# A hybrid decoder layer on one core: three ties in the order of its feed-forward tiles

## The chip, the core and the metric

The kernel runs on one core of a Trainium2 chip. Its engines are TensorE (PE in the profile, with PEld for the loading of weights into the array), VectorE (DVE), ScalarE (ACT), GpSimd (POOL) and SyncE (SP). The last two issue transfers here. The metric is the device time of one execution in microseconds (us). Three executions of the kernel before took 1223.24, 1223.34 and 1223.8 us; the median is 1223.34 us.

## What is computed

One decoder layer on 512 tokens of width 1024 in float32: a SwiGLU feed-forward (width 2816), a pair of token mixers with a gated merge, and a second SwiGLU feed-forward, each with a norm before and behind it.

```python
def swiglu(x, w_gate, w_up, w_down):
    return (jax.nn.silu(x @ w_gate) * (x @ w_up)) @ w_down

f = swiglu(rms_norm(h, ffn1_norm_pre[l]), ffn1_w_gate[l], ffn1_w_up[l], ffn1_w_down[l])
h = h + 0.5 * rms_norm(f, ffn1_norm_post[l])
u = rms_norm(h, mix_norm_pre[l])
...
h = h + rms_norm(merged @ w_out[l], mix_norm_post[l])
f = swiglu(rms_norm(h, ffn2_norm_pre[l]), ffn2_w_gate[l], ffn2_w_up[l], ffn2_w_down[l])
h = h + 0.5 * rms_norm(f, ffn2_norm_post[l])
```

The change touches the first feed-forward and the entry into the second; the mixers between them stay as they are.

## The kernel before

**Products.** Every operand is split into a high and a low part (`split`, lines 268 to 270: ACT copies the high part, DVE subtracts it for the low part), and a product of two operands is three matmuls: high by high, high by low, low by high. The 22 tiles of 128 feed-forward columns are numbered f. The first 6 (in the second feed-forward the first 3) are computed directly (`std`). Each of the others is computed by `prod` (line 994): gate and up weights against the two halves of the tokens form a two by two block product that needs seven products instead of eight, p1, p5, p6, p2, p7, p3, p4 in this order, with 12 matmuls of 256 columns each (lines 1008 to 1010). The weights of a tile come as one transfer (`raw`) and are summed and split by `w_forms_in_place` (line 646) into four tiles: p1 and p2 share one, p7 and p5 another, p6 and p3 a third, p4 has its own.

**Banks.** In `prod`, `b` is the accumulator bank of p1, p6, p7 and p4 (bank 0 for even f, bank 1 for odd f), `y` is bank 2 and `z` is bank 5. Behind p1, ACT copies b into y (line 1029); behind p5 it copies z away as `c5` and behind p6 b as `c6` (line 1016). p3 adds onto z and must wait until c5 was read; DVE then forms the two sums of line 1021: for the up half, b behind p7 plus c5 (the **up sum**), and for the gate half, z behind p3 plus c6 (the **gate sum**). p4 adds onto b and must wait for the up sum.

**Down parts.** The product with the down weights is computed in groups of four tiles, again by seven products, here called down parts: `step` (line 913) runs one of them, 12 matmuls of 512 columns (lines 922 to 924) in two halves of 6, on banks 3 and 4 or 6 and 7. `ffn_order` (line 55) places them behind tiles; in the first feed-forward the table `LEAD` (line 26) puts three down parts in a row (p1, p2, p5) behind tiles 7 and 10, and two behind tiles 8, 9, 11 and 12. The weights of a down part are brought by `supply` (line 885) on POOL's queue into `npair` or into one of two `dr` tiles, and split into `wd` by `down_form` (line 897). For p6 and p3 the transfer adds onto what `npair` holds, so it can only be issued once the part before it in `npair` was split. In `prod`, the splits for the coming down parts are tied behind the last ACT copy, c6 (`with behind("copy")`, line 1037).

**What sets the order.** The program is recorded in the order of the code and then put in order by priorities; a high priority pulls an instruction ahead. `behind(...)` (line 987) ties the instructions recorded inside it behind the last one noted for an engine in the dictionary `last`. p1 of every tile is tied behind the last PE instruction recorded before (line 1024), a down part likewise; p5 and p3 are not tied and can be pulled ahead. The weight forms of a coming tile (`prep`) are tied behind DVE's and ACT's last noted instructions; the dictionary is empty when a feed-forward starts.

**Between the feed-forwards.** The last product of the mixers (`last_product`, line 439) works on four blocks of 128 tokens. For each, `Boundary.block` (line 473) computes the new h, its squared sum on ACT (line 478), the root with a few operations on single columns (lines 390 and 342 to 344) and the normed rows u (line 483). `Boundary.turn` (line 487) transposes u on PE (line 491), and ACT and DVE split it into the inputs of the second feed-forward (lines 494 to 496). `gemm_first` (line 305) runs the first five direct products of the second feed-forward, first for the first 256 tokens, then for the others; `turn(2)` stands behind its third product and `turn(3)` behind its fourth.

Of the kernel before, what the change touches and what calls it, by code (L numbers as in the profile page):

```python
# [10 lines left out]
F32 = mybir.dt.float32  # L11
F32R = mybir.dt.float32r
AF = mybir.ActivationFunctionType
# [12 lines left out]
LEAD = {7: (0, ("p1", "p2", "p5")), 8: (0, ("p6", "p7")), 9: (0, ("p3", "p4")),  # L26
        10: (1, ("p1", "p2", "p5")), 11: (1, ("p6", "p7")), 12: (1, ("p3", "p4"))}
# [127 lines left out]
def hybrid_layer(ctx: ExitStack, tc: tile.TileContext, xT: bass.AP, xN: bass.AP, wst: bass.AP,  # L155
                 first: bass.AP, rows: bass.AP, wdn: bass.AP, wbig: bass.AP, consts: bass.AP, bias: bass.AP, out: bass.AP):
    nc = tc.nc
    DVE, ACT, PE = nc.vector, nc.scalar, nc.tensor
# [30 lines left out]
    def fb(b, sl=slice(0, D)):  # L189
        return facc[:, 2 * b:2 * b + 2, :].rearrange("p k t -> p (k t)")[:, sl]  # L190
# [219 lines left out]
    FHALVES = (slice(0, T), slice(T, D))  # L410
# [54 lines left out]
    class Boundary:  # L465
# [21 lines left out]
        def turn(self, b):  # L487
            for i, u in enumerate(self.u.pop(b)):
                ps = aux_ps()
                for j in range(4):  # L490
                    PE.transpose(ps[:, j * P:(j + 1) * P], u[:, j * P:(j + 1) * P], ident)
                src = ps.rearrange("p (k t) -> p k t", k=4)
                hi, lo = (t[:, :, b * P:(b + 1) * P] for t in (self.his[i], self.los[i]))
                ACT.activation(hi, src, AF.Copy)
                DVE.tensor_sub(lo, src, hi.bitcast(F32))
                ACT.activation(fb(b, FHALVES[i]), ps, AF.Copy)

    def act_of(his, los):
        return Act([his[k // 4][:, k % 4, :] for k in range(8)], [los[k // 4][:, k % 4, :] for k in range(8)])
# [57 lines left out]
    def forms_of(x, his, los, pool, copied, places={}):  # L557


        spool[0] = pool  # L560
        fx = facc.rearrange("p k t -> p (k t)").rearrange("p (b c) -> p b c", b=4)

        def quarter(i, j):
            return fx[:, 2 * j:2 * j + 2, i * T:i * T + T]

        def slot():
            return tx_slot(pool, 1 if copied else 2).rearrange("p s k t -> p s (k t)").rearrange(
                "p s (b c) -> p s b c", b=2)

        x01, x10, x11 = quarter(0, 1), quarter(1, 0), quarter(1, 1)  # L570
        t, d = {}, {}
        for name, i, j in (("p1", 0, 0), ("p2", 1, 0), ("p3", 1, 1)):
            t[name] = tuple(z[i][:, :, HALVES[j]] for z in (his, los))

        def copies():
            for name in ("p1", "p2", "p3"):
                v = big([P, 2, 4, HB])
                for i in range(2):
                    nc.gpsimd.dma_start(v[:, i], t[name][i])
                t[name] = v[:, 0], v[:, 1]  # L580

        def form(name, v, src):
            t[name] = tuple(v[:, i].rearrange("p b (k t) -> p k b t", k=4) for i in range(2))
            split(v[:, 0], v[:, 1], src)

        def first():
            d[1], d[2] = (pool.tile([P, 2, T], F32, name="ts", tag="s", bufs=2) for _ in range(2))
            DVE.tensor_sub(d[1], quarter(0, 0), x01)
            DVE.scalar_tensor_tensor(d[2], x11, -1.0, d[1], op0=ALU.mult, op1=ALU.subtract)
            form("p6", slot(), d[2])  # L590

        def second():
            DVE.tensor_sub(x01, x11, x01)
            form("p7", places["p7"](), x01)

        def third():
            DVE.scalar_tensor_tensor(d[2], d[2], -1.0, x10, op0=ALU.mult, op1=ALU.subtract)
            form("p4", slot(), d[2])

        def fourth():  # L600
            form("p5", places["p5"](), d[1])

        if not copied:
            return t, [first, second, third, fourth]

        def early():
            if copied:
                copies()
            d[1], d[2] = (pool.tile([P, 2, T], F32, name="ts", tag="s", bufs=2) for _ in range(2))
            DVE.tensor_sub(d[1], quarter(0, 0), x01)  # L610
            DVE.scalar_tensor_tensor(d[2], x11, -1.0, d[1], op0=ALU.mult, op1=ALU.subtract)
            DVE.tensor_sub(x01, x11, x01)

        def middle():
            form("p6", slot(), d[2])
            DVE.scalar_tensor_tensor(d[2], d[2], -1.0, x10, op0=ALU.mult, op1=ALU.subtract)
            form("p5", big([P, 2, 2, T]), d[1])

        def late():
            form("p7", big([P, 2, 2, T]), x01)  # L620
            form("p4", big([P, 2, 2, T]) if copied else slot(), d[2])

        return t, [early, middle, late]
# [189 lines left out]
        def rows(self):  # L813
            return self.ub.rearrange("p (s k) t -> p s (k t)", s=2)

    def ffn(n, x, r, forms_x, home, pss):
        t, steps = forms_x
        n0 = NSTD[n]
        ub, wdt, dr = home.ub, home.wd, home.dr
# [161 lines left out]
                    else:  # L981
                        add(u0, True)

        last = {}

        @contextmanager
        def behind(*engines):
            with ExitStack() as es:
                for e in engines:
                    if e in last:  # L990
                        es.enter_context(tc.issue_after(last[e]))
                yield

        def prod(f, w, due):

            g = tmp("g")
            b, y, z = b_of[f % 2][:, :HB], y_[:, :HB], z_[:, :HB]
            u = ub[:, f % 4, :] if 4 < f < LAST[0] or f < 4 else tmp("u")
            if n == 1 and f in (6, 8):
                u = tmp("u")  # L1000

            def product(p, ps, start):
                if len(t[p][0].shape) == 4:
                    ps = ps.rearrange("q (b t) -> q b t", b=2)
                for k in range(4):
                    ks = slice(k * P, (k + 1) * P)
                    wh, wl, xh, xl = w[p][:, 0, ks], w[p][:, 1, ks], t[p][0][:, k], t[p][1][:, k]
                    PE.matmul(ps, wh, xh, start=start and k == 0, stop=False, skip_group_check=True)  # L1008
                    PE.matmul(ps, wh, xl, start=False, stop=False, skip_group_check=True)  # L1009
                    i = PE.matmul(ps, wl, xh, start=False, stop=k == 3, skip_group_check=True)  # L1010
                last["PE"] = i.ins

            def copy(ps):
                c = tpool.tile([P, HB], F32, name="c", tag="c", bufs=CB)
                with tc.high_priority(offset=EVAC):
                    last["copy"] = ACT.activation(c, ps, AF.Copy).ins  # L1016
                return c

            def sum_of(dst, ps, c):
                with tc.high_priority(offset=EVAC):  # L1020
                    DVE.tensor_add(dst, ps, c)

            lead = f == n0
            with behind("PE"):
                product("p1", b, True)
            c1 = copy(b) if lead else None
            if not lead:
                with tc.high_priority(offset=EVAC):
                    ACT.activation(y, b, AF.Copy)
            product("p5", z, True)  # L1030
            c5 = copy(z)
            product("p6", b, False)
            c6 = copy(b)
            product("p2", y, lead)
            if lead:
                sum_of(g[:, lo_], y, c1)
            with behind("copy"):
                for a, p in due:
                    down_form(a, p)
            product("p7", b, False)  # L1040
            sum_of(u[:, hi_], b, c5)
            with tc.high_priority(offset=EVAC):
                ACT.activation(g[:, lo_], g[:, lo_] if lead else y, AF.Silu)
            product("p3", z, False)
            sum_of(g[:, hi_], z, c6)
            product("p4", b, False)
            last["ACT"] = ACT.activation(g[:, hi_], g[:, hi_], AF.Silu).ins
            with tc.high_priority(offset=EVAC):
                DVE.scalar_tensor_tensor(u[:, lo_], g[:, lo_], -1.0, b, op0=ALU.mult, op1=ALU.mult)
            last["DVE"] = DVE.scalar_tensor_tensor(u[:, hi_], g[:, hi_], -1.0, u[:, hi_], op0=ALU.mult,  # L1050
                                                   op1=ALU.mult).ins
            return u
# [76 lines left out]
        last = Act(*zip(*(last_act(f) for f in range(*LAST))))  # L1129
# [16 lines left out]
    pss = [acc_ps() for _ in range(4)]  # L1146
# [36 lines left out]
    with ExitStack() as mx:  # L1183
# [17 lines left out]
        pss = [acc_ps() for _ in range(4)]  # L1201
# [209 lines left out]
        early = dpool.tile([2 * len(AHEAD_PAIRS), P, T], F32, name="early")  # L1411
        ready = {}
        for i, (c, kind) in enumerate(AHEAD_PAIRS):
# [6 lines left out]
            f = AF.Sigmoid if kind == "sig" else AF.Gelu_apprx_tanh  # L1420
# [7 lines left out]
    with ExitStack() as mx:  # L1428
# [130 lines left out]
        for hd in range(NH):  # L1559
# [9 lines left out]
            for kind, c in FILL[hd]:  # L1569
                if kind == "attn":  # L1570
                    ws = fetch((kind, c))
                    for i in range(2):
                        ps = acc_ps()
                        gemm(ps, [w[:, i * T:(i + 1) * T] for w in ws], attn)
                        DVE.tensor_mul(facc[:, 2 * c + i, :], ps, facc[:, 2 * c + i, :])
                else:
                    ps = acc_ps()
# [10 lines left out]
        for c in range(KC):  # L1588
            ps = acc_ps()
# [7 lines left out]
    home2 = Home(ap2)  # L1597
# [8 lines left out]
    keys = [(w, 2, i) for i in range(NSTD[2]) for w in ("gate", "up")]  # L1606
    pss = gemm_first(keys[:NFIRST], u2, [home2.spare()[2]],
                     {3: [lambda: bd2.turn(2)], 4: [lambda: bd2.turn(3)]})
    end2 = ffn(2, u2, None, forms_of(u2, his, los, ap2, True), home2, pss)
    new_h()  # L1610
    for b in range(4):
        nc.gpsimd.dma_start(hb(b), kept[b])
# [132 lines left out]
```

## Time and profile before

| | |
|---|---|
| median of three executions | 1223.34 us |
| profiled execution, its own time | 1223.28 us |
| span of its instructions | 1221.2 us (2.1 us lie around it) |
| granted TensorE clock | 0.999 |
| DVE | 984.0 us busy, 81% |
| ACT | 746.0 us busy, 61% |
| raw weights, SP queue | 90 transfers of 1024 KB, 4.9 us from issue to landing (median) |
| `npair`, POOL queue | 32 transfers of 512 KB, 5.5 us (median) |
| `dr`, POOL queue | 40 transfers of 512 KB, 5.8 us (median) |

Busy shares are averages over very different stages. PE's records overlap, since a matmul is pipelined: the distance from one start to the next tells what a matmul costs, not the length of its record. Where the start-to-start distance is longer than usual, PE waited, and the bracket at the end of a row names the idle time that is left and what ended it.

### The profile page before, as it was taken

What the parts mean: (1) busy time and instruction counts of PE and PEld (TensorE: products, weight loads), DVE (VectorE), ACT (ScalarE), POOL (GpSimd) and SP (SyncE); (2) the same over time, 40 slices, a digit from 0 to 9 for tenths busy, and PEclk for the clock granted to TensorE, in tenths of its full rate; (3) what the DMA queues carried; (4) which work ended last, traced back from release to release, by engine and by line L of the source; (5) the groups of instructions that cost most, each with busy time, mean ns of one, the idle gap of its engine ahead of it and who ended that gap; (6) DMA issues with size and microseconds to landing.
All of it is one profiled execution on the core that took longest, in us unless ns stands there. A gap on an engine that the chain in (4) does not pass through costs nothing.

```text
span 1221.2 us, 19573 instructions
## 1 busy us (share of the span) xinstructions
PE 1209.9 (99%) x7790; PEld 1102.6 (90%) x7790; DVE 984.0 (81%) x1540; ACT 746.0 (61%) x1238; POOL 84.5 (7%) x139
## 2 busy tenths in 40 slices
PE   9999999999999999999999999999999999999998
PEld 8898989999878899999999888888899999999996
DVE  7998878988579888888776998755789887979864
ACT  6566665655656564666666788634566665656452
POOL 0001111100102000000001000000110110101000
PEclk9999999999999999999999999999999999999999
DMA  6336646464735222223235223524462655555441
GB/s 247 138 104 173 170 111 171 141 163 121 255 116 176 105 82 101 78 79 104 70 138 202 75 91 141 183 101 164 132 190 87 182 155 146 159 136 163 114 156 69
DMA packets 37452, 167.63 MB, mean 137 GB/s; under 512 B 4209, under 2 KB 7665, under 8 KB 25329
## 3 DMA queue, kind: packets, MB, share of 16 engines
q1 hardware_dynamic: 18432, 107.13, 25.2%
q0 software_dynamic: 18928, 59.25, 18.1%
q8 instruction: 61, 1.00, 0.3%
q14 instruction: 31, 0.25, 0.1%
HBM read 153.79 MB, written 8.39 MB: 133 GB/s over the span
## 4 chain that ended last, share of the span: by engine, by line
PE 93%; DVE 4%; issue 1%; DMA 1%; ACT 1%; DVEq 0%; ACTq 0%
PE bank L1008 10%; PE bank L1009 9%; PE bank L1010 9%; PE bank L284 7%; PE bank L286 7%; PE bank L285 7%; PE bank L675 6%; PE bank L676 6%; PE bank L677 6%; PE bank L923 4%; PE bank L922 4%; PE bank L924 4%; PE bank L405 3%; PE bank L406 3%; PE bank L404 3%; DVE w L270 1%
## 5 line engine op out<-in xcount | busy, mean ns | idle before, releaser
L270 DVE TENSOR_TENSOR w<-raw,w 128x1024 fp32r<-128x1024 f32 (+1 forms) x276 | 300.6, 1100 | 61.9 <-ACT w L269 56.0
L269 ACT ACTIVATE w<-raw 128x1024 fp32r<-128x1024 f32 (+1 forms) x276 | 258.9, 956 | 102.4 <-PE bank L286 40.1
L1008 PE MATMUL bank<-big,w 128*128 128x256 f32 x840 | 240.6, 286 | 2.5 <-ACT c L1016 0.9
L1009 PE MATMUL bank<-big,w 128*128 128x256 f32 x840 | 237.5, 283 | 0.0
L1010 PE MATMUL bank<-big,w 128*128 128x256 f32 x840 | 236.2, 283 | 0.0
L1008 PEld LDWEIGHTS bank<-big,w 128*128 128x128 f32 x840 | 160.8, 191 | 7.3 <-ACT c L1016 1.9
L1009 PEld LDWEIGHTS bank<-big,w 128*128 128x128 f32 x840 | 160.9, 192 | 1.6
L1010 PEld LDWEIGHTS bank<-big,w 128*128 128x128 f32 x840 | 160.3, 192 | 0.0
L922 PE MATMUL bank<-wd,act 128*128 128x512 f32 x224 | 87.8, 392 | 0.0
L923 PE MATMUL bank<-wd,act 128*128 128x512 f32 x224 | 87.8, 392 | 0.0
L924 PE MATMUL bank<-wd,act 128*128 128x512 f32 x224 | 87.2, 389 | 0.0
L675 PE MATMUL bank<-big,w 128*128 128x256 f32 x252 | 73.0, 290 | 0.0
L677 PE MATMUL bank<-big,w 128*128 128x256 f32 x252 | 71.5, 284 | 0.0
L676 PE MATMUL bank<-big,w 128*128 128x256 f32 x252 | 71.2, 283 | 0.0
L1016 ACT ACTIVATE c<-bank 128x256 f32<-128x256 f32 x72 | 27.5, 382 | 61.3 <-PE bank L1010 60.8
L270 DVE TENSOR_TENSOR wd<-npair,wd 128x1024 fp32r<-128x1024 f32 x24 | 29.4, 1224 | 37.7 <-ACT wd L269 37.7
L284 PE MATMUL bank<-act,w 128*128 128x512 f32 (+1 forms) x168 | 58.6, 354 | 0.0
L285 PE MATMUL bank<-act,w 128*128 128x512 f32 (+1 forms) x168 | 58.5, 349 | 0.0
L286 PE MATMUL bank<-act,w 128*128 128x512 f32 (+1 forms) x168 | 58.5, 349 | 0.0
L284 PE MATMUL bank<-big,w 128*128 128x512 f32 x144 | 56.0, 389 | 0.0
L285 PE MATMUL bank<-big,w 128*128 128x512 f32 x144 | 56.0, 389 | 0.0
L286 PE MATMUL bank<-big,w 128*128 128x512 f32 x144 | 56.0, 389 | 0.0
(399 smaller groups left out, 3208.7 us busy)
## 6 DMA issues: line engine op xcount, KB each, us to landing
raw<-in_w SPq DMA_DIRECT2D x90, 1024.0 KB, 4.9
dr<-in_wdn POOLq DMA_DIRECT2D x40, 512.0 KB, 5.8
npair<-in_wdn POOLq DMA_DIRECT2D x32, 512.0 KB, 5.5
big<-act POOLq DMA_DIRECT2D x6, 512.0 KB, 4.1
h<-in_x SPq DMA_DIRECT2D x8, 256.0 KB, 5.2
h<-in_xn POOLq DMA_DIRECT2D x4, 512.0 KB, 5.2
raw<-in_wbig SPq DMA_DIRECT2D x2, 1024.0 KB, 4.8
kept_m<-h POOLq DMA_DIRECT2D x4, 512.0 KB, 2.9
```

Of the source, the lines that this page charges most:

```text
L269: ACT.activation(dh, src, AF.Copy)
L270: DVE.tensor_sub(dl, src, dh.bitcast(F32))
L284: PE.matmul(ps, wh, xh, start=first, stop=False)
L285: PE.matmul(ps, wh, xl, start=False, stop=False)
L286: PE.matmul(ps, wl, xh, start=False, stop=last)
L675: PE.matmul(ps, wh, xh, start=start and k == 0, stop=False, skip_group_check=True)
L676: PE.matmul(ps, wh, xl, start=False, stop=False, skip_group_check=True)
L677: PE.matmul(ps, wl, xh, start=False, stop=k == 3, skip_group_check=True)
L922: PE.matmul(ps, xh, wh, start=start and k == 0, stop=False, skip_group_check=True)
L1008: PE.matmul(ps, wh, xh, start=start and k == 0, stop=False, skip_group_check=True)
L1009: PE.matmul(ps, wh, xl, start=False, stop=False, skip_group_check=True)
L1010: i = PE.matmul(ps, wl, xh, start=False, stop=k == 3, skip_group_check=True)
```

## The change

There are three edits. `Boundary.turn` notes its last DVE and ACT instructions, and the second feed-forward starts with them in its dictionary, so that the weight forms of its first two tiles (3 and 4, until tile 3 has noted its own) are tied behind the turn of the last block. In the first feed-forward, in a tile that stands behind three down parts in a row (`early`: tiles 8 and 11), p1 is no longer tied, and p3 is tied behind p7.

```diff
-                DVE.tensor_sub(lo, src, hi.bitcast(F32))
-                ACT.activation(fb(b, FHALVES[i]), ps, AF.Copy)
+                i_dve = DVE.tensor_sub(lo, src, hi.bitcast(F32))
+                i_act = ACT.activation(fb(b, FHALVES[i]), ps, AF.Copy)
+            self.last = {"DVE": i_dve.ins, "ACT": i_act.ins}
...
-    def ffn(n, x, r, forms_x, home, pss):
+    def ffn(n, x, r, forms_x, home, pss, after={}):
...
-        last = {}
+        last = dict(after)
...
-            with behind("PE"):
+            early = n == 1 and len(LEAD.get(f - 1, ((), ()))[1]) > 2
+            with behind(*(() if early else ("PE",))):
                 product("p1", b, True)
...
-            product("p3", z, False)
+            with behind(*(("PE",) if early else ())):
+                product("p3", z, False)
...
-    end2 = ffn(2, u2, None, forms_of(u2, his, los, ap2, True), home2, pss)
+    end2 = ffn(2, u2, None, forms_of(u2, his, los, ap2, True), home2, pss, bd2.last)
```

The line numbers of the changed kernel are one higher from line 497 on, two higher between lines 1027 and 1043 and three higher behind that. No instruction is added or removed but for rows that are merged in one listing and not in the other; three places change their order.

**Tile 8, on ACT.** The names: `c_969` is c5, `c_983` is c6, `bank2_75<-bank0_73` is the copy of b into y behind p1, the `s5` rows belong to the down part p5 in front of the tile. Before, in a row:

```order
L1016 ACTIVATE c_969<-bank5_78 128x256
L934 ACTIVATE s5_873<-bank6_79 128x512
L269 ACTIVATE act_96<-ub_97 128x512
L934 ACTIVATE s5_873<-bank7_80 128x512
L1029 ACTIVATE bank2_75<-bank0_73 128x256
L1016 ACTIVATE c_983<-bank0_73 128x256
L269 ACTIVATE wd1_99<-npair_95 128x1024
L269 ACTIVATE wd0_98<-dr0_100 128x1024
```

And changed:

```order
L1031 ACTIVATE bank2_75<-bank0_73 128x256
L935 ACTIVATE s5_873<-bank6_79 128x512
L935 ACTIVATE s5_873<-bank7_80 128x512
L1017 ACTIVATE c_969<-bank5_78 128x256
L269 ACTIVATE act_96<-ub_97 128x512
L1017 ACTIVATE c_983<-bank0_73 128x256
L269 ACTIVATE wd1_99<-npair_95 128x1024
L269 ACTIVATE wd0_98<-dr0_100 128x1024
```

On PE p1 now runs beside the down part where p5 ran, p5 follows, and p3, of which 5 matmuls stood in front of p1, comes whole behind p7. The two `wd` splits stand behind c6 as before.

**Tile 11, on DVE.** The names: `c_1455` is c5 and its row is the up sum, `c_1469` is c6 and its row the gate sum; `w8_1415` and `w8_1414` are weights of tile 12. Before, in a row:

```order
L1021 TENSOR_TENSOR g_1429<-bank5_78,c_1469 128x256
L270 TENSOR_TENSOR w8_1415<-raw_1411,w8_1415 128x1024
L270 TENSOR_TENSOR wd0_98<-npair_95,wd0_98 128x1024
L1021 TENSOR_TENSOR ub_97<-bank1_74,c_1455 128x256
L270 TENSOR_TENSOR w8_1414<-raw_1411,w8_1414 128x1024
L270 TENSOR_TENSOR wd1_99<-dr0_100,wd1_99 128x1024
```

And changed:

```order
L270 TENSOR_TENSOR wd0_98<-npair_95,wd0_98 128x1024
L270 TENSOR_TENSOR wd1_99<-dr0_100,wd1_99 128x1024
L1022 TENSOR_TENSOR ub_97<-bank1_74,c_1455 128x256
L270 TENSOR_TENSOR w8_1415<-raw_1411,w8_1415 128x1024
L1022 TENSOR_TENSOR g_1429<-bank5_78,c_1469 128x256
L270 TENSOR_TENSOR w8_1414<-raw_1411,w8_1414 128x1024
```

The up sum, for which p4 waits, now stands behind both `wd` splits instead of one. On PE, 11 of the 12 matmuls of tile 12's p5 stood between p7 and p4 of tile 11; now tile 11's own p3 stands there, and tile 12's p5 follows later.

**Entry of the second feed-forward, on ACT.** The names: `w4_8686` is the first weight form of tile 3, its `raw` a transfer; `h_7657` with `stat_8310` is the squared sum of the last block; the rows of line 494 are turns. Before, in a row:

```order
L383 ACTIVATE stat_8301<-stat_8298,stat_8077 128x1
L269 ACTIVATE w4_8686<-raw_8681 128x512
L478 ACTIVATE facc_87,stat_8310<-h_7657 128x1024
L494 ACTIVATE act_7926<-bank7_80 128x4x128
L390 ACTIVATE stat_8312<-stat_8310,eps_86 128x1
```

And changed:

```order
L383 ACTIVATE stat_8301<-stat_8298,stat_8077 128x1
L478 ACTIVATE facc_87,stat_8310<-h_7657 128x1024
L494 ACTIVATE act_7926<-bank7_80 128x4x128
L390 ACTIVATE stat_8312<-stat_8310,eps_86 128x1
L494 ACTIVATE act_7926<-bank5_78 128x4x128
```

The split of `w4_8686` moved from ahead of the squared sum to behind the last copy of the turn; on DVE its low part and the two sums of lines 654 and 655 moved likewise, from ahead of the root's operations of the last block to behind its turn.

## Prediction

> **What bounds the kernel now.** I read the page first, then the waits of PE, then the timelines of PE, ACT, DVE and POOL around the three places that move.
>
> ```profile
> span 1221.2 us, 19573 instructions
> PE 1209.9 (99%) x7790; PEld 1102.6 (90%) x7790; DVE 984.0 (81%) x1540; ACT 746.0 (61%) x1238; POOL 84.5 (7%) x139
> PEclk9999999999999999999999999999999999999999
> PE 93%; DVE 4%; issue 1%; DMA 1%; ACT 1%; DVEq 0%; ACTq 0%
> ```
>
> The span, the busy engines, the granted clock and the engines' shares of the chain that ended last: PE sets the time at full clock. An order that keeps every matmul can gain only where PE waits. All of PE's waits on others, from the view of waits (total, times, longest; the one left out is at the start):
>
> ```profile
> PE bank L491 <- DVE u L483: 1.4, 1, 1.4
> ...
> PE bank L1008 <- ACT c L1016: 0.9, 2, 0.5
> PE bank L1008 <- DVE u L1021: 0.9, 1, 0.9
> ```
>
> That is 3.2 us, all at the places that the edits touch. But idle time understates a wait, since a matmul's record is longer than its slot. PE's timeline in tile 8:
>
> ```profile
> 99.61 0.28 PE L1010 MATMUL bank<-big,w 128*128 128x256 f32 x1
> 100.36 0.38 PE L1008 MATMUL bank<-big,w 128*128 128x256 f32 x1 [0.47 <-ACT c L1016]
> ...
> 110.07 0.28 PE L1010 MATMUL bank<-big,w 128*128 128x256 f32 x1
> 111.27 0.39 PE L1008 MATMUL bank<-big,w 128*128 128x256 f32 x1 [0.92 <-DVE u L1021]
> 111.49 0.28 PE L1009 MATMUL bank<-big,w 128*128 128x256 f32 x1
> ```
>
> Start to start a matmul of 256 columns takes 0.12 us. p3 came 0.75 behind p5's last (0.63 lost, waiting for c5), p4 1.20 behind p7's last (1.08 lost, waiting for the up sum); behind such a restart the next one takes 0.22, 0.10 more. For whole stretches:
>
> ```profile
> 98.06:112.80 14.74, 13.35 (x96) 12.29 (x95) 12.31 (x18) 8.55 (x14) 2.29 (x3) 1.00 0.52 105
> 163.11:179.92 16.81, 16.30 (x111) 14.83 (x111) 15.92 (x24) 10.51 (x18) 1.96 (x3) 1.00 0.44 130
> 886.37:891.83 5.46, 4.04 (x35) 3.79 (x33) 4.64 (x10) 3.47 (x6) 1.29 (x2) 1.00 0.84 242
> ```
>
> The columns are length, then busy time and count of PE, PEld, DVE, ACT and POOL, then clock and transfers; a matmul across an edge counts too, and a few records are missing. Tile 8 has 84 matmuls of 0.12 us and 11 of a down part at 0.23 us in its stretch, 12.6 us; it took 14.74, so 2.1 us are waits.
>
> **Tile 8: p1 first, p3 between p7 and p4.** p1 depends on nothing that is late, so p1, p5 and the down part close up, and p4 could start at 98.06 + 72 x 0.12 + 11 x 0.23 = 109.2 instead of 111.27. What else does p4 need? The up sum, which stands on DVE behind both splits for the coming down parts:
>
> ```profile
> 107.15 0.38 ACT L1016 ACTIVATE c<-bank 128x256 f32<-128x256 f32 x1 [1.79 <-PE bank L1010]
> 107.43 1.05 ACT L269 ACTIVATE wd<-npair 128x1024 fp32r<-128x1024 f32 x1
> ...
> 108.51 1.23 DVE L270 TENSOR_TENSOR wd<-npair,wd 128x1024 fp32r<-128x1024 f32 x1 [2.31 <-ACT wd L269]
> 109.66 1.22 DVE L270 TENSOR_TENSOR wd<-dr,wd 128x1024 fp32r<-128x1024 f32 x1
> 110.79 0.42 DVE L1021 TENSOR_TENSOR u<-bank,c 128x256 f32<-128x256 f32 x1
> ```
>
> From the start of the ACT split of `npair` to p4 are 111.27 - 107.43 = 3.84 us, and neither order changes this piece. That split stands behind c6, which moves from 107.15 to about 105.0 (p6 ends 2.1 earlier). It also needs its transfer:
>
> ```profile
> 100.97 0.87 POOL L879 DMA_DIRECT2D npair<-in_wdn  x1 [4.92 <-DVE wd L270]
> npair<-in_wdn POOLq DMA_DIRECT2D x1, 512.0 KB, 5.4
> ```
>
> Issued at 100.97 behind a DVE split that the change leaves where it is (its own inputs are all ahead of the tile), it lands 5.4 later, at 106.4. So ACT starts at 106.45 instead of 107.43, with the second split, the weight splits of tile 9 and the gate's Silu queued behind it, and p4 starts at 106.45 + 3.84 = 110.3: PE still waits 1.1 us there. **Gain 1.0 us**, of the 2.1 that the removed waits promise. Bounds: 0 if the transfer takes 1 us longer, 2.1 if it doesn't bind.
>
> **Tiles 11 and 12.** Here the waits before are smaller, because 11 matmuls of tile 12's p5 filled the place between p7 and p4:
>
> ```profile
> 149.55 0.28 PE L1008 MATMUL bank<-big,w 128*128 128x256 f32 x1
> ...
> 163.11 0.39 PE L1008 MATMUL bank<-big,w 128*128 128x256 f32 x1
> ...
> 168.13 0.39 PE L1008 MATMUL bank<-big,w 128*128 128x256 f32 x1 [0.47 <-ACT c L1016]
> ```
>
> The first row is where the tile's matmuls begin among the down part's. p4 starts at 163.11 with no idle time marked. Changed, six products and the down part would bring PE to p4 at 149.55 + 72 x 0.12 + 12 x 0.23 = 160.9. But the transfer:
>
> ```profile
> 152.72 0.86 POOL L879 DMA_DIRECT2D npair<-in_wdn  x1 [6.35 <-DVE wd L270]
> npair<-in_wdn POOLq DMA_DIRECT2D x1, 512.0 KB, 6.7
> 160.22 1.05 ACT L269 ACTIVATE wd<-npair 128x1024 fp32r<-128x1024 f32 x1
> 162.63 0.42 DVE L1021 TENSOR_TENSOR ub<-bank,c 128x256 f32<-128x256 f32 x1
> ```
>
> It lands at 159.4; before, that hurt nothing, as ACT took it at 160.22 and the up sum stood behind this one split, at 162.63. Changed, the up sum stands behind both splits: 159.4 + 0.05 + 3.84 (tile 8's piece, the same five instructions) = 163.3 for p4. PE waits 2.4 us there and has not done p5's 11 matmuls, 1.3 us, which now come later. From p4's start to the next down part behind tile 12 the stretch above took 16.81. Changed it holds 96 matmuls of 256 columns and 24 of 512: 96 x 0.12 + 24 x 0.227 = 17.0, and 0.2 for restarts and for tile 12's own up sum, which by my count of DVE's rows comes just when it is needed: 17.2. So 0.2 later at the start and 0.4 longer, a **loss of 0.6 us**, though the waits at 168.13 and in front of p3 are gone. Bounds: a gain of 2.0 if the transfer doesn't bind (0.7 if it takes 5.4 as tile 8's), a loss of 4.0 if it takes 10.1, as this one in the same feed-forward:
>
> ```profile
> 129.91 0.87 POOL L879 DMA_DIRECT2D npair<-in_wdn  x1 [2.46 <-DMA npair<-in_wdn]
> npair<-in_wdn POOLq DMA_DIRECT2D x1, 512.0 KB, 10.1
> ```
>
> I take 6.7, since the transfer and all in flight beside it shift together.
>
> **Entry of the second feed-forward.**
>
> ```profile
> 880.86 1.28 DVE L475 SCALAR_TENSOR_TENSOR h<-facc,stat,h 128x1024 f32<-128x1024 f32 x1
> 883.52 0.63 ACT L269 ACTIVATE w<-raw 128x512 fp32r<-128x512 f32 x1 [4.18 <-DMA raw<-in_w]
> 884.05 1.04 ACT L478 ACTIVATE facc<-h 128x1024 f32<-128x1024 f32 x1
> 884.18 0.69 DVE L270 TENSOR_TENSOR w<-raw,w 128x512 fp32r<-128x512 f32 x1 [2.04 <-ACT w L269]
> ...
> 887.77 1.41 DVE L483 SCALAR_TENSOR_TENSOR u<-h,stat,ub 128x512 f32<-128x512 f32 x2
> ```
>
> The split of a weight that nobody needs yet holds ACT for its transfer; the last block's h is ready at 882.14, but its squared sum starts at 884.05, and DVE's three moved rows, of 0.69 each from 884.18, stand in the root's way. u is made from 887.77, and PE, which reaches the turn at 887.1, waits the 1.4 us of the second view. Changed, the sum starts at 882.2. For the block before:
>
> ```profile
> 875.39 1.10 ACT L478 ACTIVATE facc<-h 128x1024 f32<-128x1024 f32 x1
> 878.29 1.42 DVE L483 SCALAR_TENSOR_TENSOR u<-h,stat,ub 128x512 f32<-128x512 f32 x2
> ```
>
> 2.9 us from the sum to u, with one split of line 495 between; now two stand there, 0.6 more: u from 885.7, its first half at 886.45, its second at 887.1. Now the turn's first four transposes stand where the third window begins, at 886.4, and the other four straight behind them, so PE waits 0.1 at each. The stretch from 886.37 then holds 24 matmuls (2.9 us), 8 transposes at 0.11 (0.9) and some 0.4 of switching and waiting, 4.2 instead of 5.46: **gain 1.3 us**, 0.9 to 1.7 by the ends of these rows. What the moved rows cost: 2.1 us of DVE, which was idle for 2.04 us in front of them. They now follow the turn, and everything behind them on DVE, the sums of the inputs and the other weight splits, keeps its place to within a microsecond:
>
> ```profile
> 906.87 1.22 DVE L270 TENSOR_TENSOR w<-raw,w 128x1024 fp32r<-128x1024 f32 x1
> ...
> 911.70 0.28 PE L1008 MATMUL bank<-big,w 128*128 128x256 f32 x1
> ```
>
> The last split of tile 3 ends at 908.1; tile 3 starts at 911.70, at 910.4 when earlier, and needs that split only for its third product, 2.9 us on. The cover is 5 us; without it each microsecond would cost one.
>
> **Sum.** -1.0 + 0.6 - 1.3 = -1.7 on the profiled execution's 1223.28, which is the median's 1223.34 within 0.1: **1221.6 us**. A difference of 0.2%, 2.4 us, is what a measurement here can tell: 1220.9 to 1225.8 counts as no change, and the forecast is inside it, near its edge.
>
> **The rivals.**
>
> *The quick transfer.* Tile 11's `npair` lands in 5.4 as tile 8's, or another row waits less than I count. Tile 11 gains 0.7 instead of losing 0.6: 1220.3; with no transfer binding at all (2.1, 2.0 and 1.7 gained) 1217.5. For: several rows near 5.5 us; against: the 6.7 is this very transfer's row. Chance with its neighbours down to 1217.5: 0.22.
>
> *Absorbed.* DVE paces the second feed-forward, so that its entry's 1.3 us are waited for again: 1222.9. For: DVE is 81% busy and holds 4% of the chain. Against: the list of PE's waits has no row behind the entry. Chance 0.10.
>
> *Slower: the up sums behind slow transfers.* Both tiles now hold p4 behind a transfer added onto `npair`, with no other work left to fill the place. If both take 10.1 us, tile 8 loses 4.7 and tile 11 3.4 more: 1221.6 + 8.1 = 1229.7. It decides from 1.7 us longer in all (no gain left); over 0.2% slower from 4.2. For: the range 5.4 to 10.1 in one feed-forward; against: the slow one ran beside a transfer of raw weights and neither edit moves one there. Chance 0.08. [...]
>
> **How the numbers follow.** Forecast 0.60, quick 0.22, absorbed 0.10, slower 0.08. The forecast's own range is 1220.6 to 1222.6, a third of it under 1220.9: faster 0.20 + 0.22 = 0.42; same 0.40 + 0.10 = 0.50; slower 0.08. The range leaves out the slower case and the quick one's far end: 1219.2 to 1223.3.
>
> **What would show it.** In tile 8, p3 follows p7 without a gap, the wait for c5 (line 1016 before, 1017 after) is gone, and p4 waits about 1.1 us for the up sum, with ACT's split of `npair` idle until its transfer. In tile 11 p4 waits about 2.4 us for the up sum. At the entry the wait of 1.4 us on line 483 is 0.1 or gone, and the second half of the direct products starts 1.3 us sooner against the end of `gemm_first`'s fourth product. The forecast is wrong if ACT takes the `npair` splits right behind c6 (faster), if PE idles where the second feed-forward had none, or if p4 in tile 8 or 11 waits above 3 us (slower).

## The result and the profile after

The changed kernel takes 1220.7 us (median of 21 executions, 1219.85 to 1223.85) beside 1223.27 us of the kernel before (21 executions, 1222.74 to 1224.37). The ratio is 0.9982, with a 95% interval of 0.9977 to 0.9988; the medians differ by 2.6 us, where 1.7 were forecast. Ten more executions on another occasion (run e11_again below) give 1221.9 and 0.9988 [0.9979, 0.9997]. All 31 together have a median of 1220.75, and they form two groups: 22 lie at 1219.85 to 1222.09, and 9 at 1222.91 to 1224.37. The profiled execution took 1221.92 us, 1.36 less than the profiled one before.

The page's head, with the lines that the prediction showed of before (the span, the busy engines, the granted clock, the engines' shares of the chain that ended last):

```profile
span 1219.8 us, 19570 instructions
PE 1207.8 (99%) x7790; PEld 1101.7 (90%) x7790; DVE 983.5 (81%) x1540; ACT 745.9 (61%) x1238; POOL 84.3 (7%) x139
PEclk9999999999999999999999999999999999999999
PE 84%; DVE 7%; ACT 5%; issue 2%; DMA 2%; DVEq 0%; SPq 0%; ACTq 0%
```

The work is the same to 0.5 us on DVE and 0.1 on ACT, so the gain lies in waits. But DVE, ACT and DMA now hold 14% of the chain instead of 6%. The view of PE's waits (total, times, longest; the row of the kernel's start and two of 0.2 us are left out):

```profile
PE bank L1009 <- DVE u L1022: 2.7, 1, 2.7
PE bank L1009 <- DVE ub L1022: 1.1, 1, 1.1
```

Gone are the wait of 1.4 us at the entry of the second feed-forward and the two waits for c5. The wait of p4 for the up sum has grown from 0.9 to 2.7 in tile 8, and tile 11 has a new one of 1.1. The stretches of the prediction, from the same matmul to the same matmul in the changed kernel (tile 8; tiles 11 and 12 up to the next down part; the turn with the 24 matmuls behind it), with length first and granted clock ahead of the last two columns:

```profile
97.61:113.19 15.58, 12.88 (x96) 12.18 (x95) 12.40 (x18) 7.43 (x13) 2.28 (x3) 1.00 0.52 102
149.95:179.71 29.76, 28.64 (x206) 26.95 (x204) 24.17 (x36) 18.28 (x31) 2.81 (x4) 1.00 0.47 114
...
886.26:890.35 4.09, 4.06 (x35) 3.80 (x34) 3.31 (x5) 3.02 (x6) 1.29 (x2) 1.00 0.70 188
```

Tiles 11 and 12 before, as one stretch:

```profile
149.55:179.92 30.37, 29.75 (x206) 27.10 (x205) 23.73 (x35) 18.14 (x30) 2.81 (x4) 1.00 0.45 112
```

So in this execution tile 8 lost 0.84 us (15.58 beside 14.74), tiles 11 and 12 gained 0.61, and the entry gained 1.37 (4.09 beside 5.46): 1.14 of the span's 1.4. The tiles have changed signs against the forecast, and the next lines tell why. ACT, DVE and PE in tile 8, then the time from POOL's issue to the landing:

```profile
107.81 1.06 ACT L269 ACTIVATE wd<-npair 128x1024 fp32r<-128x1024 f32 x1 [2.75 <-DMA npair<-in_wdn]
108.91 1.22 DVE L270 TENSOR_TENSOR wd<-npair,wd 128x1024 fp32r<-128x1024 f32 x1 [2.57 <-ACT wd L269]
110.05 1.22 DVE L270 TENSOR_TENSOR wd<-dr,wd 128x1024 fp32r<-128x1024 f32 x1
111.18 0.42 DVE L1022 TENSOR_TENSOR u<-bank,c 128x256 f32<-128x256 f32 x1
111.66 0.39 PE L1009 MATMUL bank<-big,w 128*128 128x256 f32 x1 [2.70 <-DVE u L1022]
...
113.19 0.40 PE L923 MATMUL bank<-wd,act 128*128 128x512 f32 x1
...
npair<-in_wdn POOLq DMA_DIRECT2D x1, 512.0 KB, 7.2
```

From ACT's split to p4 are 111.66 - 107.81 = 3.85 us; 3.84 were predicted. ACT stood idle for the transfer, as predicted, but the transfer took 7.2 us where it had taken 5.4. In tile 11 it went the other way:

```profile
158.77 1.06 ACT L269 ACTIVATE wd<-npair 128x1024 fp32r<-128x1024 f32 x1 [1.17 <-DMA npair<-in_wdn]
162.61 0.39 PE L1009 MATMUL bank<-big,w 128*128 128x256 f32 x1 [1.12 <-DVE ub L1022]
...
npair<-in_wdn POOLq DMA_DIRECT2D x1, 512.0 KB, 5.6
```

Again 3.84 us from the split to p4, and the transfer took 5.6 us instead of 6.7. At the entry, ACT's squared sum, DVE's u and PE's transposes:

```profile
882.05 1.06 ACT L478 ACTIVATE facc<-h 128x1024 f32<-128x1024 f32 x1 [2.83 <-DVE h L475]
885.44 1.41 DVE L483 SCALAR_TENSOR_TENSOR u<-h,stat,ub 128x512 f32<-128x512 f32 x2
886.34 1.29 PE L491 MATMUL bank<-cst,u 128*128 128x128 f32 x8
```

The sum starts as soon as h is there, u follows 3.4 us later, and the eight transposes run in one group with no wait marked.

### The profile page after: what moved, and what is told of

The parts are those of the page before. It is cut to its first block, busy times and chain, and to the rows that moved or that the text cites. A ratio compares the mean times of both kernels' runs of the same rounds, so it can differ in the third digit from the quotient of the medians.

```text
span 1219.8 us, 19570 instructions
## 1 busy us (share of the span) xinstructions
PE 1207.8 (99%) x7790; PEld 1101.7 (90%) x7790; DVE 983.5 (81%) x1540; ACT 745.9 (61%) x1238; POOL 84.3 (7%) x139
## 4 chain that ended last, share of the span: by engine, by line
PE 84%; DVE 7%; ACT 5%; issue 2%; DMA 2%; DVEq 0%; SPq 0%; ACTq 0%
PE bank L1009 9%; PE bank L1010 9%; PE bank L1011 9%; PE bank L676 6%; PE bank L677 6%; PE bank L678 6%; PE bank L284 4%; PE bank L286 4%; PE bank L285 4%; PE bank L923 4%; PE bank L924 4%; PE bank L925 4%; PE bank L405 3%; PE bank L406 3%; PE bank L404 3%
```

## The experiments

All the kernels below change only what is shown. "After" is the changed kernel; times are medians, with the ratio to the kernel before in the same runs. That ratio lies near the ratio of the means, so a few long executions raise it where they leave the median alone.

### The parts of the change

**e1_entry: the entry tie alone.** In `prod`:

```diff
-            early = n == 1 and len(LEAD.get(f - 1, ((), ()))[1]) > 2
+            early = False
```

> The entry tie alone; the first feed-forward is that of the kernel before. Theory (the terms add up, PE paces the second feed-forward): the wait of 1.4 us on line 483 is gone, the entry is 1.3 to 1.4 us shorter and stays so to the end, 1221.9 us, with the narrow spread of before (about 1.6 us from lowest to highest). Rival (VectorE paces the second feed-forward and takes the gain back): 1223.0.

Measured: 1222.11 us (11 executions, 1221.49 to 1222.65), ratio 0.9988 [0.9979, 0.9996] beside 1223.66 before. That is 1.55 us, with 0.5 to 2.6 by the interval, and 1.37 by the stretch above. The wait on line 483 is gone, and no execution lies above 1222.65.

**e2_tiles: the tile ties alone.** In the call of the second feed-forward:

```diff
-    end2 = ffn(2, u2, None, forms_of(u2, his, los, ap2, True), home2, pss, bd2.last)
+    end2 = ffn(2, u2, None, forms_of(u2, his, los, ap2, True), home2, pss)
```

> The ties of tiles 8 and 11 alone, without the entry tie. Theory (p4 of both tiles waits for the npair transfer, ScalarE's split of it and two splits on VectorE): the rest of the change's gain, about 1.2 us in the median, 1222.1, with the wide spread of the changed kernel (4 us from lowest to highest), since the transfers' times now reach the end. Rival (all of the change's gain is the entry's, the tiles only exchange one wait for another): 1223.3.

Measured: 1222.13 us beside 1223.66, ratio 0.9996 [0.9986, 1.0007], so no change that could be told, although the median is the 1222.1 of the theory: four long executions undo it in the mean. Eight executions lie at 1220.63 to 1222.35, four at 1224.91 to 1228.1. The slowest is the profiled one; ACT and PE in its tile 11, then the granted clock (third column from the end) in stretches from there:

```profile
160.60 1.06 ACT L269 ACTIVATE wd<-npair 128x1024 fp32r<-128x1024 f32 x1 [3.07 <-DMA npair<-in_wdn]
...
164.44 0.58 PE L1009 MATMUL bank<-big,w 128*128 128x256 f32 x1 [3.02 <-DVE ub L1022]
...
161.30:164.40 3.10, 0.13 (x2) 0.00 (x0) 2.70 (x4) 3.10 (x5) 0.85 (x1) 0.86 0.00 0
164.40:165.80 1.40, 1.35 (x6) 1.36 (x7) 1.40 (x3) 0.37 (x1) 0.56 (x1) 0.50 0.69 64
168.60:170.40 1.80, 1.80 (x6) 1.41 (x5) 0.43 (x1) 0.00 (x0) 0.00 (x0) 0.50 0.90 323
170.40:172.00 1.60, 1.60 (x8) 1.30 (x8) 1.60 (x3) 0.60 (x1) 0.00 (x0) 1.00 0.95 394
```

The transfer took 7.5 us here, p4 again starts 164.44 - 160.60 = 3.84 behind the split, and PE is idle for 3.02 us. The clock falls to half some 0.9 us before the end of that wait, 2.1 us into it (0.86 in the mean of its stretch), and stays there until about 170.4, some 6.8 us in all; matmuls of 256 columns follow each other in 0.21 us instead of 0.12. The stretch of tiles 11 and 12 took 34.37 us, 4.0 more than before and 4.6 more than in the first profile of after. Of the 4.6, 1.9 lie ahead of p4 (164.44 - 149.88 = 14.56 us beside 162.61 - 149.95 = 12.66), where the transfer is late, and 2.7 behind it, at half clock.

**e6_tile8 and e7_tile11: the tile ties in one tile each, with the entry tie.**

```diff
-            early = n == 1 and len(LEAD.get(f - 1, ((), ()))[1]) > 2
+            early = n == 1 and f == 8
```

and the same with 11.

> The change with its tile ties in tile 8 alone (entry tie kept, tile 11 as before). Theory: the entry gives 1.4 us, and tile 8 gives 1.0 where its transfer onto npair takes 5.4 us, 0 at 6.4 and a loss of 0.8 at 7.2; with the 5.4 to 7.2 of the profiles so far the median is 1.4 to 2.0 us below the kernel before (about 1221.8 for 1223.5), and the spread is small, since p4 of tile 8 waits 2.9 us at the most so far, under what halved the clock in tile 11. Rival (the gain of the tiles is all tile 8's, the prediction's sizes): 2.4 us below, about 1221.1, and tile 11 alone loses 0.6.

> The change with its tile ties in tile 11 alone (entry tie kept, tile 8 as before). Theory: the entry gives 1.4 us, and tile 11 gives 0.6 to 0.7 where its transfer takes about 5.5 us, so most executions lie 2.0 us below the kernel before (about 1221.5 for 1223.5); an execution in which the transfer takes 7.5 has p4 idle for 3 us, the clock halves for 6.8 us, and it lies some 4 to 5 us higher: a few of the runs stand apart at 1225 or above, and none between. Rival (the prediction's size, a loss of 0.6 at a transfer of 6.7): 0.7 below, about 1222.8, with no second group.

Measured beside 1223.36 before: e6_tile8 1222.14 us, ratio 0.999 [0.9982, 0.9999], eight executions at 1220.9 to 1222.48 and three at 1223.72 to 1224.32; e7_tile11 1221.44 us, ratio 0.9984 [0.9975, 0.9993], ten at 1220.32 to 1222.29 and one at 1223.91. Against the entry alone neither tile adds a gain in the median that its interval can tell from none. Both have a second group: that tile 8 would have none was wrong, and tile 11's lies at 1223.91, not at 1225 or above. The profiled executions fell in the first group. Tile 8's stretch and p4 in e6_tile8, with its transfer, which took 5.5 us:

```profile
98.01:111.92 13.91, 12.87 (x97) 12.19 (x96) 12.40 (x18) 7.42 (x13) 2.28 (x3) 1.00 0.61 118
...
110.39 0.38 PE L1009 MATMUL bank<-big,w 128*128 128x256 f32 x1 [1.04 <-DVE u L1022]
...
npair<-in_wdn POOLq DMA_DIRECT2D x1, 512.0 KB, 5.5
```

With 5.5 us the tile gains 14.74 - 13.91 = 0.83, and p4 waits 1.04, close to the forecast's 1.0 and 1.1. In e7_tile11 the stretch of tiles 11 and 12 took

```profile
150.51:180.23 29.72, 28.65 (x206) 26.94 (x204) 24.18 (x36) 18.29 (x31) 2.81 (x4) 1.00 0.47 115
```

a gain of 0.65 where the trace has 5.6 us from issue to landing.

**e10_p3_only: p1 tied as before, p3 tied in tiles 8 and 11.**

```diff
-            with behind(*(() if early else ("PE",))):
+            with behind("PE"):
                 product("p1", b, True)
```

> The changed kernel with p1 of tiles 8 and 11 tied as before; p3 stays tied behind p7. p6 then follows p1 directly and waits some 0.7 us for the copy of b. Theory (p4's start is set by the npair transfer and what follows it): that wait is hidden ahead of p4, so that freeing p1 is worth nothing here; 1220.7 us, the same wide spread as the changed kernel, and the same 3.85 us from ScalarE's split of npair to p4. Rival (the free p1 carries the gain of these tiles): about 1222.1, like the entry tie alone, or 0.7 us per tile worse than the changed kernel.

Measured: 1220.87 us, ratio 0.9979 [0.9971, 0.9988], a median as after's (1220.75), but without the wide spread that was expected: none of the 11 executions lies above 1222.36. The waits of PE in its profile, but for the start and one of 0.2 us:

```profile
PE bank L924 <- DVE wd L270: 1.3, 2, 0.7
PE bank L1009 <- ACT bank L1031: 1.3, 3, 0.5
```

Freeing p1 adds nothing to the median that can be told; with the tie of p3 alone it is the same. But the way there differs from the theory. In both tiles PE now waits earlier, in the down part for DVE's split of `wd` and in front of p6 for the copy of b, and none of its waits is in front of p4. In tile 8 ACT takes the `npair` split at 106.48, right behind c6 and with no wait for the transfer (5.9 us from 100.43), and p4 follows 3.83 us later, at 110.31, just as PE arrives. p7 ends 1.5 us later here than in after (last start at 110.19 instead of 108.67), so a late transfer would leave p4 a shorter wait. That this keeps the second group away is not shown, only that there is none in these 11 executions.

**e11_again: after, profiled a second time.**

> The changed kernel itself, profiled a second time. Theory: the transfers onto npair in tiles 8 and 11 vary between executions of one kernel, so they land after other times than 7.2 and 5.65 us, and p4 starts 3.85 us behind the start of ACT's split of npair whatever they are. Rival: the times belong to the order of the kernel, and come out as 7.2 and 5.65 again within 0.2.

Measured: 1221.9 us, ratio 0.9988 [0.9979, 0.9997]; five executions at 1219.91 to 1220.9 with a mean clock of 0.999 to 1.0, and five at 1222.91 to 1224.37 with 0.997. The profiled one, 1224.37, is of the upper group. Its p4 in tile 8, the down part behind it, and the granted clock from there:

```profile
112.68 0.39 PE L1009 MATMUL bank<-big,w 128*128 128x256 f32 x1 [2.80 <-DVE u L1022]
...
115.15 0.63 PE L923 MATMUL bank<-wd,act 128*128 128x512 f32 x1
115.58 0.63 PE L924 MATMUL bank<-wd,act 128*128 128x512 f32 x1
...
npair<-in_wdn POOLq DMA_DIRECT2D x1, 512.0 KB, 7.3
...
109.70:112.60 2.90, 0.18 (x2) 0.00 (x0) 2.67 (x4) 2.90 (x4) 0.86 (x1) 1.00 0.01 3
112.60:113.50 0.90, 0.82 (x5) 0.82 (x6) 0.90 (x2) 0.40 (x2) 0.56 (x1) 0.72 0.82 64
113.50:114.50 1.00, 1.00 (x6) 1.00 (x6) 1.00 (x3) 0.38 (x2) 0.00 (x0) 0.50 0.66 98
114.50:115.50 1.00, 1.00 (x5) 0.98 (x5) 0.76 (x2) 1.00 (x3) 0.00 (x0) 0.50 1.03 197
115.50:117.00 1.50, 1.50 (x6) 1.14 (x5) 1.50 (x3) 0.52 (x1) 0.00 (x0) 0.70 1.09 289
```

The transfer took 7.3 us, near the first profile's 7.2 (as the rival has it for this tile; tile 11's 5.5 beside 5.6 too), and p4 starts 3.85 us behind ACT's split at 108.83, as the theory has it. Yet the whole ran 2.45 us longer than in the first profile. 0.94 of it are there before the transfer's issue (101.47 beside 100.53); for the rest, the clock fell to half behind PE's idle time of 2.80 us, and behind the 2.70 in the first profile it did not. The clock rows add up to 3.4 us at half (0.5 us of the second stretch, all from 113.5 to 115.5, 0.9 of the last but one). From p4's start to the next down part are 115.15 - 112.68 = 2.47 us, where the first profile had 113.19 - 111.66 = 1.53, and the first three matmuls of that down part took 0.43 us each (115.15 to 115.58 is the first) instead of 0.23: 0.94 + 0.6 = 1.5 us for the half clock.

### The cause of p4's wait

**e4_no_load: after, without p6's transfers onto `npair` in the first two groups.** In `supply`, this share of the down weights is left out of the sum:

```diff
+                if n == 1 and a < 2 and p == "p6":
+                    continue
```

> The changed kernel without the npair transfers of the down parts p6 of the first two groups of the first feed-forward, in the same order of instructions; it leaves out that share of the down weights, and two transfers of 512 KB. Theory (the transfer is what is late): ScalarE splits npair right behind c6, p4 of tile 8 comes at most 0.2 us late and p4 of tile 11 not at all; 1217.8 and a narrow spread. Rival (the two splits on VectorE alone make the up sum late): p4 still waits 1 to 3 us in both tiles, 1220.7.

Measured: 1217.9 us (1217.42 to 1218.91), ratio 0.9956 [0.9943, 0.9969]. p4's waits are gone but for 0.2 us in tile 8, where it starts 0.31 us behind p7's last matmul instead of 0.12. The prediction had 1217.5 for the case that no transfer binds. The run also takes 1024 KB off the queue, and what that alone is worth was not measured.

**e9_double: after, with the same transfers issued twice.**

```diff
-            for i, q in enumerate(qs):
+            for i, q in enumerate(qs * 2 if n == 1 and a < 2 and p == "p6" else qs):
```

> The changed kernel, with the npair transfer of down part p6 issued twice, one behind the other, in the first two groups of the first feed-forward; that share of the down weights is then added twice. Theory: each of the two waits of p4 grows by one transfer of about 5.5 us to 6.5 us or more, 11 us in all, and as both waits are then longer than 3 us, TensorE restarts at half clock in both tiles and loses 3.4 us more in each: 1220.7 + 11 + 6.8 = 1238.5. Rival (the half clock of one earlier profile was chance): 1231.7 and a clock row of 1.00 behind both waits.

Measured: 1230.07 us (two executions), ratio 1.0054 [1.0035, 1.0072], 9.4 over after. The rival's 1231.7 lies in the interval and the theory's 1238.5 doesn't, but the number tells neither, since the second transfer changed the order as well: the scheduler now put the split of `npair` behind the up sum on DVE. DVE and PE around the end of tile 8, and the granted clock:

```profile
108.44 0.41 DVE L1022 TENSOR_TENSOR u<-bank,c 128x256 f32<-128x256 f32 x1
113.51 1.23 DVE L270 TENSOR_TENSOR wd<-npair,wd 128x1024 fp32r<-128x1024 f32 x1 [4.65 <-ACT wd L269]
...
113.53 0.50 PE L923 MATMUL bank<-wd,act 128*128 128x512 f32 x1 [2.92 <-ACT wd L269]
114.79 0.80 PE L924 MATMUL bank<-wd,act 128*128 128x512 f32 x1 [0.77 <-DVE wd L270]
...
114.80:116.20 1.40, 1.40 (x3) 1.16 (x4) 1.40 (x3) 1.10 (x2) 0.86 (x1) 0.50 0.00 0
```

p4 went ahead with almost no wait, and the down part behind the tile waited for the weights themselves, 2.92 and 0.77 us, at half the clock behind that. In tile 11 the same waits were 2.37 and 0.76. So this run doesn't measure the price of a transfer in front of p4. It shows that the sum ahead of the split frees p4 from the transfer, and where the next bound lies.

### The sum ahead of the splits

**e3_sum_first: after, in tiles 8 and 11 the up sum ahead of both `wd` splits.**

```diff
             def sum_of(dst, ps, c):
                 with tc.high_priority(offset=EVAC):
-                    DVE.tensor_add(dst, ps, c)
+                    last["sum"] = DVE.tensor_add(dst, ps, c).ins
...
+            first = early
             with behind("copy"):
-                for a, p in due:
+                for a, p in () if first else due:
                     down_form(a, p)
             product("p7", b, False)
             sum_of(u[:, hi_], b, c5)
+            with behind("copy", "sum"), tc.high_priority(offset=EVAC):
+                for a, p in due if first else ():
+                    down_form(a, p)
```

> The changed kernel, and in tiles 8 and 11 the up sum stands ahead of both wd splits on VectorE. Theory: the waits of p4 (2.7 and 1.1 us in the changed kernel's profile) are gone, about 3 us less than the changed kernel, 1217.7, and the spread is narrow again. Rival (the splits only become late for the down parts behind the tile, so that PE waits there instead): 1220.7 and PE waits in lines 923 to 925 behind p4.

Measured: 1219.99 us (1219.16 to 1220.94, no upper group), ratio 0.997 [0.9959, 0.9981]. p4's waits in tiles 8 and 11 are gone, but the time is 2.3 us above the theory and nearer to the rival's. The rival's own waits, in lines 923 to 925, are not there. Others came up: in tile 13 0.5 us for c5 in front of a free p3 and 0.4 for an up sum, and 0.4 for an up sum ahead of tile 8, at 81.73.

**e8_p3_tied: e3_sum_first, and p3 tied behind p7 in every tile.**

```diff
-            with behind(*(("PE",) if early else ())):
+            with behind("PE"):
                 product("p3", z, False)
```

> The up sum first in tiles 8 and 11, and p3 tied behind p7 in every tile, so that the order of tile 13, which the up sum first alone had disturbed (waits of 0.6, 0.2 and 0.6 us there), is as in the changed kernel. Theory: 1.5 us less than with the up sum first alone, 5.0 us less than before, about 1218.5 beside 1223.5, with a narrow spread. Rival (p3 pulled ahead was of use elsewhere): 1220 or more.

Measured: 1218.18 us (1218.11 to 1219.91), ratio 0.9959 [0.9947, 0.9972] beside 1223.6: 0.3 under the theory.

**e5b_all_tied: e8_p3_tied, with the up sum first in every tile of both feed-forwards** (`first = early` becomes `first = True`).

> As the one before, and the up sum stands ahead of the wd splits in every tile of both feed-forwards. Theory: the waits for the up sum at tiles 14 and 5, 9, 13 of the second feed-forward (0.40 us each with the restart, rows at 210, 956, 1016 and 1076 us of the profile before) are gone too: 1.6 us less, about 1216.9 beside 1223.5. Rival (the splits come too late for the down parts behind the tiles, where two follow each other on the same transfer): 1218.5 or more, with PE waiting in lines 923 to 925.

Measured: 1216.37 us (1215.51 to 1217.72), ratio 0.9943 [0.9929, 0.9956]: faster than both kernels, 7.2 us under the kernel before. DVE in its tile 8, and all of PE's waits but the one at the start:

```profile
107.73 0.42 DVE L1022 TENSOR_TENSOR u<-bank,c 128x256 f32<-128x256 f32 x1 [1.42 <-PE bank L1011]
108.20 1.23 DVE L270 TENSOR_TENSOR wd<-npair,wd 128x1024 fp32r<-128x1024 f32 x1
...
PE bank L923 <- ACT w L269: 0.4, 1, 0.4
```

The up sum waits for p7 alone and PE never for the sum, although tile 11's transfer took 7.0 us in this profile.

**e12_sum_alone: e5b_all_tied without the ties** (p1 tied and p3 free, as in the kernel before; the entry tie stays).

> The version with the up sum ahead of the splits in every tile, but without any tie of p1 and p3 of the change: p1 tied and p3 free as before, the entry tie kept. Theory: the sum ahead of the splits takes away p4's waits, 1.1 us in tile 8 and nothing in tile 11, and the entry 1.4, while the waits for c5 in front of the free p3 (0.6 us at tile 8 and again behind tile 11, and their likes elsewhere) stay: 1220.0 to 1221.0 beside 1223.5 for the kernel before, 4 us above the version with all ties. Rival (the order of DVE's sums is the whole gain, and the ties of the change add nothing to it): 1216.4, as the version with all ties.

Measured: 1221.38 us, ratio 0.998 [0.9971, 0.9989] beside 1223.73, 0.4 above the upper end of the expectation and far from the rival. Its waits of PE:

```profile
PE bank L1009 <- ACT c L1017: 1.2, 3, 0.5
...
PE bank L1009 <- DVE g L1022: 1.0, 1, 1.0
PE bank L1009 <- DVE ub L1022: 0.8, 2, 0.5
```

A free p3 still waits for c5. The order of the sums alone is worth 2.35 - 1.37 = 1 us beyond the entry, which the interval (1.3 to 3.5 us for both) can hardly tell from none. With the ties as well it is 5 us more (1216.37). The fourth version, p3 tied in every tile without the sums first, was not run, so how these 5 us divide between the ties and the two together stays open.

## Why the prediction was right, and where it was not

**Right: the entry.** 1.3 us forecast, 1.37 measured in the stretch, 1.55 by e1_entry. The moved rows cost nothing, and the rival by which DVE takes the gain back fell: PE has no wait behind the entry that it hadn't before.

**Right: what holds p4.** The transfer onto `npair`, ACT's split, DVE's two and the up sum make one piece: from the split to p4 3.84 us were predicted, and it came out as 3.84 to 3.85 in tile 8 and in tile 11, in the two profiles of after and in e2_tiles. Without the transfers (e4_no_load) the time falls to 1217.9; with the sum ahead of the splits (e3_sum_first) the waits go as well. That p1 first is what wins time in tile 8 is not borne out: with p1 tied (e10_p3_only) the median is the same.

**Mis-sized: both tile terms, in opposite directions.** The step that failed is the reading of each transfer's time from the one profile of before as if it belonged to the place: 5.4 for tile 8, and "I take 6.7" for tile 11. In the profiles with the tie in the tile, tile 8's transfer took 5.3 (e5b_all_tied, e8_p3_tied) to 7.3 us (e11_again); tile 11's 5.5 (e11_again) to 7.5 (e2_tiles). At like times the terms hold: tile 8 gained 0.83 at 5.5 (1.0 forecast at 5.4), and lost 0.84 at 7.2, where the forecast's bound (0 for 1 us more) gives a loss of 0.8; tiles 11 and 12 gained 0.61 and 0.65 at 5.6, near the 0.7 that the prediction gave for 5.4. The loss of 0.6 that the sum carried for 6.7 was not seen, nor was a transfer of that length in front of it. One bound of the prediction doesn't follow from its own rows: with no transfer binding in tile 11, p4 comes 163.11 - 160.95 = 2.2 us sooner and the stretch behind it is 0.4 longer, a gain of 1.8 and not of 2.0, and 1217.7 in place of 1217.5.

**The size in all.** The median of 1220.7 lies between the forecast's 1221.6 and the 1220.3 of the rival with the quick transfer at tile 11. Its condition, 5.4 to 5.6 us there, is what the profiles of after, e7_tile11 and e11_again show; the slow transfer in tile 8 is in both profiles of after, and how often it comes in other executions isn't known. That the whole came out near the forecast is in part luck: in the first profile a loss of 0.84 stands where a gain of 1.0 was forecast and a gain of 0.61 where a loss of 0.6 was, and the two errors largely cancel. With the quick transfers in both tiles (0.83 in e6_tile8, 0.65 in e7_tile11) and the entry's 1.37 the sum would be 2.85, an estimate from these stretches, beside the median's 2.6; ten executions on the other occasion gave 1.5.

**Not weighed: the clock.** No term of the prediction's sum stands for a lower clock behind a wait, though the forecast has p4 wait for 2.4 us in tile 11. A single transfer of 7.3 to 7.5 was enough: PE idle for 2.80 us (e11_again) and 3.02 us (e2_tiles) and then at half clock for about 3.4 and 6.8 us, at a cost of 1.5 us in the first and 2.7 in the second. An edge in the length can't be read from these runs: in e2_tiles the clock fell 2.1 us into the wait, and in e11_again 3.1 us behind its start, when PE was running again. The theory of e9_double has 3 us and a loss of 3.4 us per tile for this; no run shows either as a rule. The figures near them are e2_tiles' wait of 3.02 us and half of its 6.8 us at half clock, beside the 2.7 us measured there, and e9_double itself had 6.8 us at half clock in tile 8 and 3.4 in tile 11, behind other waits than those of p4. That the 9 upper executions of after come from the half clock is shown for one of them by its profile. For the rest it is argued from their mean clock, 0.997 in eight of the nine (0.998 in the other) and 0.998 to 1.0 in the 22 of the lower group.

**Fallen: slower.** Neither tile's transfer took 10.1 us, and the lists of waits show no p4 above 3.02 us.

**Open.** Why the transfers vary. The ties of tile 8 are not needed for it: in e7_tile11, where tile 8 is that of before, its transfer took 7.1 us. In tile 8 the longer times (7.1 to 7.3 us) come with late landings of the three `dr` transfers ahead of them in POOL's queue (a median of 7.5 to 7.6 us, beside 6.1 in the profile of before with its 5.4), which points at the queue as a whole, but no run changed that alone. Nor is it known whether profiling lengthens them: the profiled executions of e2_tiles, e3_sum_first and e11_again are the slowest of theirs, that of e1_entry the fastest.

## What to carry to other kernels

When a tie takes away filler between two products, ask what the second one waits for in the end: here a sum of 0.4 us stood in the queue behind splits that waited for a transfer, and moving the sum ahead of them took the transfer off the path. Beyond the entry's gain the sums first in every tile brought about 1 us (1221.4), the ties in tiles 8 and 11 about as much (1220.7), and both in every tile nearly 6 (1216.4). A transfer's time from one profile is a sample: take its range over all like transfers before an edit puts it on the critical path. And a wait in front of matmuls can cost more than its length: here 1.5 us more with 2.80 us of it (e11_again), 2.7 more with 3.02 (e2_tiles), and nothing more with 2.70 (the first profile of after).

## What the hardware showed

- The clock fell to half with idle times of PE of 2.80 (e11_again), 2.92 (tile 8 of e9_double) and 3.02 us (e2_tiles), for about 3.4, 6.8 and 6.8 us, and not behind 2.70 (after). The granted clock of tile 8 in e9_double was 0.68 in the mean from 113.5 to 114.8, 0.50 from there to 118.0, 0.53 to 121.0 and 1.00 to 123.0.
- Two waits of nearly one length in one kernel, 2.70 us (after) and 2.80 (e11_again), cost nothing more and 1.5 us more. What decides between them is not shown.
- In tile 11 of e9_double PE waited 2.37 us, ran one matmul, waited 0.76, and the clock fell behind that, although each of the two waits is shorter than the 2.70 us of after. It was 0.90 in the mean from 171.2 to 172.2, 0.50 to 173.5, 0.52 to 175.5 and 1.00 to 177.0, some 3.4 us at half in all.

```profile
169.97 0.50 PE L923 MATMUL bank<-wd,act 128*128 128x512 f32 x1 [2.37 <-ACT wd L269]
171.22 0.50 PE L924 MATMUL bank<-wd,act 128*128 128x512 f32 x1 [0.76 <-DVE wd L270]
...
171.20:172.20 1.00, 0.97 (x4) 0.81 (x5) 1.00 (x2) 0.66 (x2) 0.62 (x1) 0.90 0.00 0
172.20:173.50 1.30, 1.30 (x5) 1.01 (x4) 1.12 (x3) 1.30 (x3) 0.24 (x1) 0.50 0.71 50
```

- One and the same transfer of 512 KB onto `npair` took 5.3 to 7.3 us in tile 8 over the profiles of the kernels that issue it.
